# Two pairs of projection groups of a hybrid encoder layer as seven block products each, ahead of the attention heads

## The chip, the cores and the metric

The kernel runs on one core of one Trainium2 chip. The metric is the device time of one execution in microseconds (us). Its engines have one instruction queue each and start their instructions in the order of the program: TensorE (PE) multiplies matrices and writes PSUM, VectorE (DVE) and ScalarE (ACT) work element by element and read PSUM, GpSimd (POOL) works element by element on SBUF, and SyncE (SP) issues most DMAs. An instruction that waits for another engine holds up all that stand behind it in its own queue.

## The reference: what is computed

The layer takes x (512 tokens, 1024 channels, float32), normalises it, and multiplies it with one wide matrix `w_in` whose columns belong to two token mixers and two merge gates.

```python
h = rmsnorm(x, norm_w)
proj = jnp.einsum('bsd,de->bse', h, w_in) + b_in
(mq, mk, mv, mi, mf, mo, mz, sq, sk, sv, sz, gates) = jnp.split(proj, split_at, axis=-1)
# A: matrix memory, 4 heads of 256: causal conv + silu on mq, mk; chunkwise recurrence with
#    gates mi, mf; per-head rms norm; times sigmoid(mo) * silu(mz)            -> y_m
# B: stick-breaking attention, 8 heads of 128: rms norm on sq, sk per head;
#    a = sigmoid(z) * prod(1 - sigmoid(z) of the keys between), strictly causal;
#    a @ sv, times silu(sz)                                                   -> y_s
g_m, g_s = jnp.split(jax.nn.sigmoid(gates), 2, axis=-1)
merged = g_m * (y_m @ w_proj_m) + g_s * (y_s @ w_proj_s)
x = x + merged @ w_out
```

All of it is float32. The kernel keeps that accuracy by splitting each operand of a product into a high part in the fp32r type and a low remainder, and by adding three products: high-high, high-low and low-high.

## The kernel before

**Units.** All dense products are cut into 118 units, which one loop at the end of the function runs in order (L1263). A unit of `w_in` has 512 KB of weights: 1024 rows by 128 columns for a group whose result has channels on partitions (`chan_group`, L132), or 256 rows by 512 columns for a token-major group (`tok_group`, L148), in which four units add up to four token blocks of 128 by 512 in four PSUM banks. Either way a unit is 24 matmuls with 512 moving columns. Token-major groups are the q, k and V of the stick-breaking sets (two sets of four heads, `SbSet`) and the V of the matrix-memory pairs (`MPair`). The first four units (q of set 0) run with a code of their own (L1208), token block by token block, while x is still being normalised and transposed into `hh` and `hl`, the high and low parts of h, with 8 slices of 128 channels by 512 tokens each.

**What an iteration c of the loop does, in this order:** take the list `later[c]`; evacuate unit c-1; run the functions of the list; `ahead(c)`, which splits the weights of all units up to c+2 (ACT copies the high part, DVE subtracts to get the low part, L96) and lets SP load those up to c+4; first half of the matmuls of unit c; one step of each active head, and the start of a head that is due; second half of the matmuls. `AHEAD, LOADS = 2, 4` set the two distances. In iterations 1 to 3 the split comes first. Since every engine keeps program order, the place in this list is the place in each queue.

**later and defer.** `later[c]` holds what has been put off to iteration c, in the order in which it was entered; `defer(n, fn)` enters fn n iterations on. Three constants place the gate work: `gates_prep` (L575) fills the stationary tile `wg` on DVE in iteration 2, `gates` (L583) issues 16 matmuls against `wg` in iteration 4, before unit 4, and `gates_scan` starts in iteration 35.

**Heads.** A head is a generator that is advanced one step an iteration, except in the iterations of `REST`. Attention heads start in the iterations of `SB_START`, matrix heads in those of `M_START`, and not before their keys are done.

**q and k of a set.** The evacuation adds the bias row (L364); then `norm` takes four squares with a sum on ACT and the reciprocal root on POOL (L274, L275); k is scaled on DVE (L386) an iteration later. `turn` (L399) transposes 32 by 32 blocks on DVE, an iteration later `move` issues 16 DMAs (for set 0 all on SP, L415) which put the blocks in place, and two iterations after that q is weighted (L419).

**Buffers.** Tiles take buffers by tag; the numbers are in `BUFS` (L70). Those that matter here: `stg` 3 (loaded weights), `wh` and `wl` 3 each (split weights), `A` 4 and `P5` 2 (4 KB a partition each), `acc` 1 (2 KB, also the scratch of the squares), `tmp` 2, `qk` 9, `vl` 5, `y` 16.

**The tail.** The last product, with `w_out`, already runs as seven block products of two units each (`Product`, L1039). These halves have 12 matmuls of 512 columns.

Of the kernel before, what the change touches and what calls it, by code (L numbers as in the profile page):

```python
# [8 lines left out]
F32 = mybir.dt.float32  # L9
# [26 lines left out]
def tile_hybrid_layer(  # L36
# [157 lines left out]
    later = {}  # L194
    now = [0]

    def defer(n, fn):
        later.setdefault(now[0] + n, []).append(fn)

# [66 lines left out]
    def bias(ct):  # L266
        return bvec[:, ct:ct + 1]
# [68 lines left out]
    class SbSet:  # L336
        def __init__(self, s):
            self.s = s
            self.raw = {"q": [], "k": []}
            self.r = []  # L340
            self.v = []
            self.tz = {}

        def z_group(self):
            def evac(ct, ps):
# [9 lines left out]
        def qk_group(self, name, c0):  # L355
            row = []

            half = []

            def evac(tb, ps):  # L360
                if tb % 2 == 0:
                    half.extend(two("qk", name=name + "raw"))
                t = half[tb]
                nc.vector.tensor_tensor(t, ps, row[0], op=OP.add)  # L364
                self.raw[name].append(t)

                def norm():
                    ssq = tiny.tile([128, 4], F32, name="ssq", bufs=2)
                    rr = tiny.tile([128, 8], F32, name="r" + name, bufs=8 if name == "q" else 4)
                    r = rr[:, 0:4]  # L370
                    junk = blk("acc", BF, (128,), name="sqj")
                    for h in range(4):
                        nc.scalar.activation(junk, t[:, h * 128:(h + 1) * 128], AF.Square,
                                             accum_out=ssq[:, h:h + 1])
                    rstd(r, ssq, 128, EPS)
                    if name == "q":
                        rn = rr[:, 4:8]
                        nc.gpsimd.tensor_scalar(rn, r, -1.0, None, op0=OP.mult)
                        self.r.append((r, rn))
                        if tb == TB - 1:  # L380
                            defer(1, lambda: self.turn(name, 0))
                    else:
                        def scale():
                            for h in range(4):
                                hs = slice(h * 128, (h + 1) * 128)
                                nc.vector.tensor_scalar(t[:, hs], t[:, hs], r[:, h:h + 1], None, op0=OP.mult)  # L386
                            if tb == TB - 1:
                                done.add(("k", self.s))
                                defer(1, lambda: self.turn(name, 1))
                        defer(1, scale)  # L390

                if tb < 2 or name == "q" and self.s == 0:
                    norm()
                else:
                    defer(1, norm)

            tok_group(w_in, c0 + 512 * self.s, h_sta, evac, name == "q" and self.s == 0, c0 + 512 * self.s, row)

        def turn(self, name, g):  # L399

# [24 lines left out]
                defer(2, lambda: self.turn(name, 1))  # L425


        def v_group(self):
            row = []

            def evac(tb, ps):
                t = blk("tmp")
                nc.vector.tensor_tensor(t, ps, row[0], op=OP.add)
                vh = blk("vh", FR, (576,))[:, 0:512]
                vl = blk("vl", FR)
                nc.scalar.activation(vh, t, AF.Copy)
                self.v.append((vh, vl))
                if tb == TB - 1:
                    done.add(("v", self.s))
                return lambda: nc.vector.tensor_tensor(vl, t, vh.bitcast(F32), op=OP.subtract)  # L440

            tok_group(w_in, C_SV + 512 * self.s, h_sta, evac, False, C_SV + 512 * self.s, row)

        def head(self, h):
            hs = slice(h * 128, (h + 1) * 128)
# [136 lines left out]

    def gates():  # L583
        def row(name, p=4):
            return blk("y", name=name, p=p)

        wg = wg_t[0]
        ps = att_ps()
        for k in range(KT):
            nc.tensor.matmul(ps, wg[:, k, :], hh[:, k, :], start=k == 0, stop=False)  # L590
# [78 lines left out]
    class MPair:  # L669
# [25 lines left out]
        def qk_group(self, name, c0, o):  # L695
# [36 lines left out]

            chan_group(w_in, c0 + 512 * self.p, 512, h_mov, evac, lambda: self.prev())

        def v_group(self):
            row = []

            def evac(tb, ps):
                t = blk("tmp", shape=(2, 256))
                nc.vector.tensor_tensor(t, ps.rearrange("p (h e) -> p h e", h=2),  # L740
                                        row[0].rearrange("p (h e) -> p h e", h=2), op=OP.add)

                vh = blk("vh", FR, (576,))
                vl = blk("vl", FR, (2, 256))
                nc.gpsimd.memset(vh[:, 256:258].bitcast(F32), 1.0)
                dh = vh[:, 0:516].rearrange("p (h e) -> p h e", h=2)[:, :, 0:256]
                nc.scalar.activation(dh, t, AF.Copy)
                self.v.append((vh, vl))
                return lambda: nc.vector.tensor_tensor(vl, t, dh.bitcast(F32), op=OP.subtract)

            tok_group(w_in, C_MV + 512 * self.p, h_sta, evac, False, C_MV + 512 * self.p, row)

# [109 lines left out]
    sets = [SbSet(0), SbSet(1)]  # L862
    pairs = [MPair(0), MPair(1)]
    sets[0].qk_group("q", C_SQ)
    sets[0].qk_group("k", C_SK)
    sets[0].v_group()
    sets[0].z_group()
    sets[1].qk_group("q", C_SQ)
    sets[1].qk_group("k", C_SK)
    sets[1].z_group()  # L870
    sets[1].v_group()
    for p in pairs:
        p.o_group()
        p.z_group()
        p.v_group()
        p.qk_group("q", C_MQ, 0)
        p.qk_group("k", C_MK, 8)

    gs_t, gm_t = [], []

    def gs_tile(ct):
        if ct < 4:
# [3 lines left out]
            gs_t.extend(two("qk", name="gs"))  # L886
        return gs_t[ct]

    def gm_tile(ct):
        if ct % 2 == 0:  # L890
            gm_t.extend(two("qk", name="gm"))
        return gm_t[ct]

    def gate_group(c0, o, tile_of):
        def evac(ct, ps):
            nc.scalar.activation(tile_of(ct), ps, AF.Sigmoid, bias=bias(o + ct))

        chan_group(w_in, c0, D, h_mov, evac)

    gate_group(C_GS, 48, gs_tile)  # L900
    gate_group(C_GM, 40, gm_tile)
    n_gates = len(units)

    big = {}
# [330 lines left out]
    for p in (0, 1):  # L1235
        for h in range(2):
            pend.append((M_START[2 * p + h], 1,
                         lambda p=p: ("mk", p) in done, lambda p=p, h=h: pairs[p].head(h)))

    for k in range(5):  # L1240
        later.setdefault(n_gates - 1, []).append(y_early(k))
    for k in range(5, 8):
# [94 lines left out]
```

## Time and profile before

| what | value |
|---|---|
| median of 3 runs | 689.87 us (689.57 to 690.43) |
| profiled execution, first instruction to last (span) | 687.8 us; the page gives no other time of it |
| around the span, against the median | 2.1 us |
| granted TensorE clock | 1.000 |
| TensorE busy (matmuls) | 681.0 us, 99% |
| VectorE busy | 467.2 us, 68% |
| ScalarE busy | 337.1 us, 49% |
| GpSimd busy | 111.7 us, 16% |
| DMA | 84.74 MB, mean 123 GB/s |

Busy times are sums over one execution. A group of instructions stands as line, engine, operation, output and inputs by the program's names, and their shapes, then the count, the busy time, the mean of one in ns, and the idle time of the engine ahead of them with what ended most of it. Line numbers are those of the kernel before. Matmuls overlap: a duration of 0.39 us reaches into the next matmul, and the distance of two starts tells the rate.

### The profile page before, as it was taken

To read this page: it belongs to the slowest core of one execution; us is meant where nothing else is said; L and a number is where in the kernel's file an instruction comes from. 1 tells how busy PE (TensorE), PEld (TensorE's weight loads), DVE (VectorE), ACT (ScalarE), POOL (GpSimd) and SP (SyncE) were. 2 spreads that over 40 slices of the span, in tenths; PEclk is the share of its full clock that TensorE was granted. 3 is DMA by queue.
4 is the path that set the end of the run, shared out by engine and by line. 5 is a ranking of instruction groups with operands and counts; after the bars stand their busy time and mean duration, and the time that the engine had idled before them with its cause. 6 is when DMAs were issued, how large, how long until landed. Compare 5 with 4: busy or idle time off the path is not lost.

```text
span 687.8 us, 9389 instructions
## 1 busy us (share of the span) xinstructions
PE 681.0 (99%) x3162; PEld 568.9 (83%) x3162; DVE 467.2 (68%) x819; ACT 337.1 (49%) x631; POOL 111.7 (16%) x266
## 2 busy tenths in 40 slices
PE   8999999999999999999999999999999999999997
PEld 5888888888888888888888888888888888888876
DVE  6746787777997886789834648994352364445997
ACT  6245465566455653344466533448554343344451
POOL 4122042365430310000001210000112000111020
PEclk9999999999999999999999999999999999999999
DMA  7433543435463533643341343434223456599333
GB/s 250 139 95 107 160 138 105 134 112 149 134 171 86 124 111 83 139 95 92 107 117 53 107 109 85 128 91 134 68 64 90 115 176 200 141 206 205 121 82 103
DMA packets 122289, 84.74 MB, mean 123 GB/s; under 512 B 19018, under 2 KB 105956, under 8 KB 122240
## 3 DMA queue, kind: packets, MB, share of 16 engines
q1 hardware_dynamic: 119600, 77.97, 40.3%
q0 software_dynamic: 2496, 6.03, 4.7%
q8 instruction: 25, 0.41, 0.2%
q14 instruction: 24, 0.20, 0.1%
q10 hardware_dynamic: 144, 0.13, 0.1%
HBM read 66.22 MB, written 2.15 MB: 99 GB/s over the span
## 4 chain that ended last, share of the span: by engine, by line
PE 98%; DVE 1%; DMA 1%; SPq 0%; issue 0%; ACT 0%
PE dps L92 28%; PE dps L93 27%; PE dps L94 27%; PE aps L93 3%; PE aps L94 3%; PE aps L92 3%; PE dps L1216 1%; PE dps L1217 1%; PE dps L1218 1%; PE aps L811 1%; PE aps L813 1%; PE aps L812 1%; DMA stg<-in_w_in_dram 1%; PE aps L305 0%; DVE hl L317 0%; PE aps L591 0%
## 5 line engine op out<-in xcount | busy, mean ns | idle before, releaser
L98 DVE TENSOR_TENSOR wl<-stg,wh 128x1024 fp32r<-128x1024 f32 x92 | 112.5, 1223 | 106.0 <-ACT wh L97 105.5
L92 PE MATMUL dps<-hh,wh 128*128 128x512 f32 x448 | 175.0, 391 | 0.0
L94 PE MATMUL dps<-hh,wl 128*128 128x512 f32 x448 | 174.4, 389 | 0.0
L93 PE MATMUL dps<-hl,wh 128*128 128x512 f32 x448 | 174.4, 389 | 0.0
L97 ACT ACTIVATE wh<-stg 128x1024 fp32r<-128x1024 f32 x92 | 96.8, 1052 | 64.5 <-PE dps L94 44.3
L94 PEld LDWEIGHTS dps<-hh,wl 128*128 128x128 f32 x448 | 84.1, 188 | 17.7
L93 PEld LDWEIGHTS dps<-hl,wh 128*128 128x128 f32 x448 | 84.2, 188 | 16.8
L92 PEld LDWEIGHTS dps<-hh,wh 128*128 128x128 f32 x448 | 84.1, 188 | 16.7
L92 PE MATMUL dps<-wh,hh 128*128 128x512 f32 x224 | 87.7, 392 | 0.0
L94 PE MATMUL dps<-wh,hl 128*128 128x512 f32 x224 | 87.3, 390 | 0.0
L93 PE MATMUL dps<-wl,hh 128*128 128x512 f32 x224 | 87.2, 389 | 0.0
L94 PEld LDWEIGHTS dps<-wh,hl 128*128 128x128 f32 x224 | 42.0, 188 | 9.0
L92 PEld LDWEIGHTS dps<-wh,hh 128*128 128x128 f32 x224 | 42.1, 188 | 8.3
L93 PEld LDWEIGHTS dps<-wl,hh 128*128 128x128 f32 x224 | 42.1, 188 | 8.2
L704 DVE SCALAR_TENSOR_TENSOR acc<-tmp,vec,acc 128x511 f32<-128x511 f32 (+2 forms) x48 | 36.0, 750 | 1.7
L707 ACT ACTIVATE tmp<-acc 128x512 f32<-128x512 f32 x16 | 10.1, 633 | 50.8 <-DVE acc L704 50.8
L480 POOL TENSOR_SCALAR_AFFINE_SELECT om<-om 128x128 f32<-128x128 f32 x32 | 15.3, 479 | 96.2 <-ACT om L478 96.1
L486 DVE TENSOR_TENSOR_SCAN om<-om 128x512 f32<-128x512 f32 (+3 forms) x32 | 26.7, 834 | 5.5 <-POOL om L480 5.5
L764 POOL TENSOR_SCALAR_AFFINE_SELECT w_all<-om 128x128 f32<-128x128 f32 x16 | 5.3, 363 | 144.4 <-DMA om<-rb_d 144.4
L478 ACT ACTIVATE om<-aps,rq 128x512 f32<-128x512 f32 (+3 forms) x32 | 16.8, 524 | 21.0 <-PE aps L94 21.0
L94 PE MATMUL dps<-yh,wl 128*128 128x512 f32 x64 | 24.9, 389 | 0.0
L92 PE MATMUL dps<-yh,wh 128*128 128x512 f32 x64 | 24.9, 389 | 0.0
(249 smaller groups left out, 1217.8 us busy)
## 6 DMA issues: line engine op xcount, KB each, us to landing
stg<-in_w_in_dram SPq DMA_DIRECT2D x87, 512.0 KB, 3.9
az<-ay SPq DMA_DIRECT2D x128, 40.0 KB, 2.9
stg<-in_w_proj_s_dram SPq DMA_DIRECT2D x8, 512.0 KB, 4.7
B<-in_w_out_dram SPq DMA_DIRECT2D x8, 512.0 KB, 6.6
stg<-in_w_proj_m_dram SPq DMA_DIRECT2D x8, 512.0 KB, 5.9
wl<-stg POOLq DMA_DIRECT2D x8, 512.0 KB, 5.9
tz<-ty SPq DMA_DIRECT2D x72, 32.0 KB, 1.9
brow<-in_b_in_dram SPq DMA_DIRECT2D x8, 256.0 KB, 4.5
```

What stands on the lines that cost most here:

```text
L92: nc.tensor.matmul(ps, ah, bh, start=first, stop=False)
L93: nc.tensor.matmul(ps, ah, bl, start=False, stop=False)
L94: nc.tensor.matmul(ps, al, bh, start=False, stop=last)
L97: nc.scalar.activation(hi, src, AF.Copy)
L98: nc.vector.tensor_tensor(lo, src, hi.bitcast(F32), op=OP.subtract)
L478: nc.scalar.activation(om[:, 0:n], zp, AF.Sigmoid, scale=rn[:, h:h + 1])
L480: nc.gpsimd.affine_select(out=om[:, ts], in_=om[:, ts], compare_op=OP.is_gt, fill=1.0, base=0, channel_multiplier=1, pattern=[[-1, 128]])
L486: nc.vector.tensor_tensor_scan(back, back, back, 1.0, op0=OP.mult, op1=OP.bypass)
L704: nc.vector.scalar_tensor_tensor(acc[:, j:], t[:, 0:T - j], cw(3 - j, ch), acc[:, j:], op0=OP.mult, op1=OP.add)
L707: nc.scalar.activation(t, acc, AF.Sigmoid)
L811: nc.tensor.matmul(nm[:, 0:258], ph, vh, start=j == 0, stop=False)
L812: nc.tensor.matmul(sum_v, ph, vl, start=False, stop=False)
```

## The change

Four token-major groups leave their places: k and V of set 0, V of set 1, and V of matrix pair 0. They are taken two and two: (k of set 0, V of set 0) and (V of set 1, V of pair 0). A pair multiplies h with two blocks of 512 columns. With h cut into two halves of tokens and two of channels, and the weights into two halves of rows and the two column blocks, that is a product of 2 by 2 blocks, and the Winograd form computes it with seven block products in place of eight. Each block product is two units (`Half`) of 12 matmuls, so a pair has 14 units where there were 8 of 24. Both pairs run as units 4 to 31, ahead of the rest; E = 32.

- The sums of h (S1 to S4) are made once: `form_sum(2, i)` in iterations 2 and 3, S3 on POOL in 3 and 4, S1's split in 4 and 5, S3's split in 4 and 5, S4 in 6 and 7. The four weight blocks X, Z, Y, V of a pair are loaded in halves on SP, and the weight sums T2 and T1 (DVE), T3 and T4 (POOL) are made in place.
- Products accumulate on one another in PSUM where that gives the sums. A result that is needed twice is copied by ACT and added by a POOL DMA onto a tile that a DMA has filled with the bias row; the other part is added by DVE.
- The second pair's results go to DRAM (`v_park`) and come back 19 to 22 and 31 to 34 iterations after E. The first half of the gate group GM moves from the end to a place after z of set 1, and its results go to DRAM and back as well.
- The gate matmuls move from iteration 4 to 3; their preparation stays in iteration 2 and is entered in `later[2]` behind the form sum. The turns of q and k of set 0 get fixed places: iterations E - 7, E - 5 (by the deferral of 2) and E - 3. Heads start from E on.

```diff
+PAIRS = 2
+E = 4 + 14 * PAIRS
-SB_START = [10, 13, 16, 20, 26, 28, 32, 34]
-M_START = [52, 56, 70, 76]
-GATES_PREP, GATES_START, GATES_SCAN = 2, 4, 35
+SB_START = [E + n for n in (0, 2, 5, 8, 14, 16, 20, 22)]
+M_START = [E + n for n in (36, 40, 54, 60)]
+GATES_PREP, GATES_START, GATES_SCAN = 2, 3, E + 22
-REST = {11, 16, 20, 23, 24, 32, 44, 64}
+REST = {E + n for n in (4, 8, 11, 12, 48)}
...
+    def by_plan(s, name, fn):
+        if s:
+            defer(1, fn)
+        else:
+            later.setdefault(E + {"q": -7, "k": -3}[name], []).append(fn)
...
+    def form_sum(f, i):
+        if i == 0 and f != 3:
+            form_tiles(f)
+        if f == 2:
+            s1, t = flat("vl", "s1"), flat("acc", "st")
+            nc.vector.tensor_tensor(s1, h_part(hh, 1, 0, i), h_part(hh, 1, 1, i), op=OP.add)
+            nc.vector.tensor_tensor(t, h_part(hl, 1, 0, i), h_part(hl, 1, 1, i), op=OP.add)
+            nc.vector.tensor_tensor(s1, s1, t, op=OP.add)
+            s2 = flat("om", "s2")
+            nc.vector.tensor_tensor(s2, s1, h_part(hh, 0, 0, i), op=OP.subtract)
+            nc.vector.tensor_tensor(s2, s2, h_part(hl, 0, 0, i), op=OP.subtract)
+            sums[1, i] = s1
+            form_split(2, i, s2)
+        elif f == 1:
+            form_split(1, i, sums.pop((1, i)))
+        elif f == 3:
+            s3, t = flat("vl", "s3"), flat("tmp", "st")
+            nc.gpsimd.tensor_tensor(s3, h_part(hh, 0, 0, i), h_part(hh, 1, 0, i), op=OP.subtract)
...
+        else:
+            s4 = flat("acc", "s4")
...
+    class Half:
+        def load(self):
+            pass
+        def split(self):
+            self.wh = blk("wh", FR, (2, 512))
+            self.wl = blk("wl", FR, (2, 512))
+            name = {1: "X", 2: "Z", 6: "X", 5: "X", 7: "Y", 3: "V", 4: "Z"}[self.p]
+            split(self.pair.raw[name, self.g], self.wh, self.wl)
+        def mm(self, tb):
...
+            for i in range(2):
...
+                for n, (a, w) in enumerate(((sh, self.wh), (sh, self.wl), (sl, self.wh))):
+                    nc.tensor.matmul(pr.bank[key, tb], a, w[:, i, :], start=begin and n == 0,
+                                     stop=end and n == 2, skip_group_check=again)
...
+    class Pair:
...
+            b = self.base = len(units)
+            for p in (1, 2, 6, 5, 7, 3, 4):
+                for g in range(2):
+                    units.append(Half(self, p, g))
+            first = b == 4
+            for g in range(2):
+                if first:
+                    plan = {"X": g, "Z": g, "V": 1 + 2 * g, "Y": 2}
+                else:
+                    plan = {"X": b - 8 + g, "Z": b - 8 + 6 * g, "V": b - 4 + g, "Y": b - 6 + g}
+                for name, c in plan.items():
+                    self.at(c, self.load, name, g)
+                self.at(b + g, self.t3, g)
+                self.at(b + 1 + g, self.t2, g)
+                self.at(b + 2 + g, self.t4, g)
+                self.at(b + 4 + g, self.t1, g)
...
+        def put(self, key, q):
+            for tb in range(2):
+                u = blk("tmp", name="u")
+                nc.scalar.activation(u, self.bank[key, tb], AF.Copy)
+                nc.gpsimd.dma_start(out=self.dst[q][:, tb, :], in_=u, accum_op=OP.add)
+        def add(self, key, q):
+            for tb in range(2):
+                t = self.dst[q][:, tb, :]
+                nc.vector.tensor_tensor(t, self.bank[key, tb], t, op=OP.add)
+                self.got[q % 10](2 * (q // 10 - 1) + tb, t)
...
+    Pair(C_SK, C_SV, to_norm(0, "k"), to_parts(0))
+    Pair(C_SV + 512, C_MV, to_dram(0), to_dram(1))
...
+    for i in range(2):
+        at_unit(2 + i, form_sum, 2, i)
+        at_unit(3 + i, form_sum, 3, i)
+        at_unit(4 + i, form_sum, 1, i)
+        at_unit(6 + i, form_sum, 4, i)
...
+    for tb in range(TB):
+        at_unit(E + 19 + tb, from_dram, 0, tb, sets[1].v_parts)
+        at_unit(E + 31 + tb, from_dram, 1, tb, lambda tb, t: pairs[0].v_parts(tb, t)())
...
+    chan_group(w_in, C_GM, 512, h_mov, gm_early)
...
+    at_unit(n_gates + 3, gm_back)
+    for i in range(2):
+        at_unit(4 + i, s3_split, i)
```

More of the change, by code (lines that the diff above doesn't have):

```diff
@@ L584, in row @@
         def row(name, p=4):
-            return blk("y", name=name, p=p)
+            return blk("tmp", name=name, p=p)
         wg = wg_t[0]
@@ L864, in tile_hybrid_layer, with form_tiles, h_part, flat @@
     sets[0].qk_group("q", C_SQ)
-    sets[0].qk_group("k", C_SK)
-    sets[0].v_group()
+    form = {}
+    def form_tiles(f):
+        form[f] = [[blk("y", FR, (2, 256), name="form") for _ in range(2)] for _ in range(2)]
+        return form[f]
+    def h_part(t, row, col, i):
+        k = 4 * col + 2 * i
+        return t[:, k:k + 2, 256 * row:256 * row + 256].bitcast(F32)
+    sums = {}
+    def flat(tag, name):
+        return blk(tag, shape=(516 if tag == "om" else 512,), name=name)[:, 0:512].rearrange("p (k t) -> p k t", k=2)
@@ new lines, in to_norm, with to_parts, to_dram, from_dram @@
+    def to_norm(s, name):
+        return lambda tb, t: defer(1, lambda: sets[s].norm(name, tb, t))
+    def to_parts(s):
+        return lambda tb, t: defer(1 + tb % 2, lambda: sets[s].v_parts(tb, t))
+    v_park = [dp.tile([T, 512], F32, name="v_park") for _ in range(2)]
+    def to_dram(n):
+        return lambda tb, t: nc.sync.dma_start(v_park[n][128 * tb:128 * tb + 128, :], t)
+    def from_dram(n, tb, fn):
+        t = blk("brow", name="vback")
+        nc.sync.dma_start(t, v_park[n][128 * tb:128 * tb + 128, :])
+        later.setdefault(now[0] + 1, []).insert(0, lambda: fn(tb, t))
```

237 lines of the change are left out of this document (167 added, 70 removed).

## The prediction

> **What bounds the kernel now.** I read the page first, then busy times by stretch, then the timelines of the first 60 us.
>
> ```profile
> span 687.8 us, 9389 instructions
> PE 681.0 (99%) x3162; PEld 568.9 (83%) x3162; DVE 467.2 (68%) x819; ACT 337.1 (49%) x631; POOL 111.7 (16%) x266
> PE 98%; DVE 1%; DMA 1%; SPq 0%; issue 0%; ACT 0%
> ```
>
> TensorE bounds it: 99% busy, and 98% of the chain of waits. The page gives the profiled execution no time but its span, 687.8; the median of the runs is 689.87, so 2.1 us lie around the span, and I add them at the end.
>
> ```profile
> 14.30:37.00 22.70, 22.70 (x109) 18.66 (x108) 18.78 (x47) 7.17 (x26) 6.31 (x11) 1.00 0.35 107
> 180.00:200.00 20.00, 20.00 (x101) 17.03 (x100) 17.97 (x34) 10.89 (x20) 10.08 (x26) 1.00 0.51 140
> 640.00:660.00 20.00, 20.00 (x88) 16.06 (x87) 18.56 (x32) 12.01 (x20) 1.77 (x2) 1.00 0.28 77
> ```
>
> Columns: stretch, length, then busy us of PE, weight load, DVE, ACT, POOL, then clock. Even with DVE at 90% (17.97, 18.56 of 20) PE stands nowhere. So removed matmuls are time gained, unless something new makes PE wait.
>
> ```profile
> 1.50 4.11 PE L1184 MATMUL dps<-idle 128*128 128x512 f32 x9 [1.50 <-DVE idle L1179]
> 29.39 0.50 PE L1216 MATMUL dps<-fh,hh 128*128 128x512 f32 x1
> 34.98 0.39 PE L590 MATMUL aps<-hh,wg 128*128 128x512 f32 x1
> 38.61 0.39 PE L92 MATMUL dps<-wh,hh 128*128 128x512 f32 x1
> 44.05 0.39 PE L92 MATMUL dps<-wh,hh 128*128 128x512 f32 x1
> ```
>
> A duration (0.39) overlaps the next; starts count. One unit of 24 matmuls takes 44.05 - 38.61 = 5.44 us, 0.227 each; the 16 gate matmuls take 38.61 - 34.98 = 3.63.
>
> **What is removed.** Each pair of groups was 8 units of 24 (192 matmuls) and becomes 14 halves of 12 (168). Two pairs save 48 x 0.227 = **10.9 us**. This is firm: counts are in the code, and PE had no gaps.
>
> **What is added.** A half lasts 2.72 us but needs the same 128x1024 split as a whole unit:
>
> ```profile
> L98 DVE TENSOR_TENSOR wl<-stg,wh 128x1024 fp32r<-128x1024 f32 x92 | 112.5, 1223 | 106.0 <-ACT wh L97 105.5
> L97 ACT ACTIVATE wh<-stg 128x1024 fp32r<-128x1024 f32 x92 | 96.8, 1052 | 64.5 <-PE dps L94 44.3
> L386 DVE TENSOR_SCALAR kraw<-kraw,rk 128x128 f32<-128x128 f32 x32 | 6.6, 283 | 0.0
> L440 DVE TENSOR_TENSOR vl<-tmp,vh 128x512 fp32r<-128x512 f32 x8 | 5.5, 686 | 0.4
> L419 DVE TENSOR_SCALAR tz<-tz,qkw 128x1024 f32<-128x1024 f32 x4 | 3.0, 752 | 0.8 <-DMA tz<-ty 0.4 <-DMA stg<-in_w_in_dram 0.4
> ```
>
> In DVE starts (next fence) a 1024-wide operation costs 1.13 and a 512-wide one 0.61. Between unit 2 and unit E = 32 DVE gets 30 splits (33.9), 8 weight sums (9.0), 16 additions to the results (9.8), the form sums and their splits (24 x 0.61 = 14.6), and the rest of q, k, V and the gates, about 15 (half of the k and V rows, 3.3 and 2.7; turns and their weights, 5.6; additions of q and gate work, 3.4): 82 us. PE needs 5.44 + 3.63 + 28 x 2.72 = 85. DVE is thus nearly as full as PE, and a split is issued only two units (5.4 us) ahead: whatever makes DVE wait makes PE wait. I follow three places.
>
> **Place 1, the gates.** The gate matmuls move from unit 4 to unit 3, ahead of its matmuls in PE's order. They read `wg`, which DVE fills in the preparation at unit 2. That preparation was registered after the new form sum of unit 2, so DVE runs it behind five sums and a split.
>
> ```profile
> 28.53 1.13 DVE L317 SCALAR_TENSOR_TENSOR hl<-aps,nw_t,hh 128x128 fp32r<-128x128 f32 x4
> 29.57 1.21 DVE L98 TENSOR_TENSOR wl<-stg,wh 128x1024 fp32r<-128x1024 f32 x1
> 30.70 0.68 DVE L364 TENSOR_TENSOR qraw<-dps,brow 128x512 f32<-128x512 f32 x1
> 31.31 0.17 DVE L579 CAST wg<-gst 128x32 fp32r<-128x32 f32 x1
> 31.83 0.19 DVE L580 TENSOR_TENSOR wg<-gst,wg 128x32 fp32r<-128x32 f32 x1
> 31.48 0.31 ACT L373 ACTIVATE sqj<-qraw 128x128 bf16<-128x128 f32 x1 [6.17 <-DVE wg L579]
> 33.00 0.19 ACT L373 ACTIVATION_READ_ACCUMULATOR sqj<-qraw 128x1 f32 x1
> ```
>
> Nothing changes up to 31.31, since the sums need `hl`, finished at 29.57. Then: the first sum to 31.92; the second writes the only buffer of `acc`, which the four squares hold until 33.2; four sums to 35.65; ACT's copy (0.62) to 36.3, the low part to 36.9, the preparation (0.6, as 31.31 to 31.9 now) to 37.5. PE stands ready at 29.4: a stall of 8.1 us. Without the wait for `acc` and without hand-over times it is 6.8; with half a microsecond at each of three hand-overs 9.5. I take **8.1**.
>
> After it PE may restart slowly. The first row of the PE fence shows 9 matmuls after idleness at 0.457 each, double the later spacing. At that rate nine matmuls cost 2.1 more; at the warm rate none. A gap of 8 us is nearer the idle start than the gaps of up to 1 us in the trace, so **2.1**, with 0 to 2.1 for the range.
>
> The Trainium skill, "TensorE: Matmul & The Clock Gate", Part 1, says the clock halves after an idle window of some 3.4 us and recovers after as much activity, which speaks against any change that makes PE stand. By that page an estimate is 1.7 us here in place of 2.1. The half rate itself shows in the trace only at the start.
>
> **Place 2, pair 1.** PE leaves the gates at 37.5 + 3.6 + 2.1 = 43.2, unit 3 at 48.7, units 4 and 5 at 54.1. Unit 6 waits 0.4 for its split.
>
> ```profile
> L373 ACT ACTIVATE sqj<-qraw 128x128 bf16<-128x128 f32 x32 | 9.9, 310 | 19.1 <-DVE qraw L364 12.0 <-DVE wg L579 6.2
> L275 POOL TENSOR_TENSOR rq<-rq,mhalf 128x4 f32<-128x4 f32 x8 | 8.2, 1029 | 0.7
> 8.79 2.56 POOL L1166 TENSOR_TENSOR fl<-stg,fh 128x512 fp32r<-128x512 f32 x2 [2.57 <-ACT fh L1161]
> ```
>
> Unit 7's split stands on ACT behind the split of S3's second half, whose three sums are on POOL, behind Y's subtraction (T3) and behind the q norm of unit 3. From 48.7: q addition 0.65, four squares 1.75, POOL's norm 1.6 (1.03 is the power), T3 at 1024 wide 2.5 (twice the 1.28 of a POOL row), three sums 3.85: 59.0. Then ACT 0.62 and 1.05, DVE 1.15: 61.9. PE was ready at 57.2: 4.7. After that DVE's own queue sets the pace, against 2.72 a half:
> - unit 6 queues T2 (1.13), three sums for S4 (1.83), a split of 512 (0.62 + 0.61), then the split of unit 8 (0.4 more of ACT, 1.13): 5.7, loses 3.0;
> - unit 7 the same without T2, 4.6: 1.9;
> - units 8 and 9: T1 (1.13), ACT 1.05 and 1.13; then T1, two additions and 1.13: 3.3 and 3.5, lose 1.4;
> - unit 10: ACT has two copies and two norms (1.1 + 3.5) before its split: 2.7.
>
> With unit 6 and 0.1 at unit 11: 0.4 + 4.7 + 3.0 + 1.9 + 1.4 + 2.7 + 0.1 = **14.2**. Low end: DVE's bare work in units 4 to 11 (8 splits, 4 weight sums, 15 operations of 0.61, 8 k scalings at 0.21) is 24.4 against PE's 21.8: 2.6. High end: POOL half as slow again and each hand-over a little late, 20. Slow restarts at the shorter gaps are taken as nothing. The second pair has no form sums; its units come to 2 to 4 us of DVE with a lead of 5.4, and I charge nothing (if it falls behind as pair 1 did from unit 8, 4).
>
> **Place 3, the seam at unit 32.** The turns of q and k are fixed at units 25, 27 and 29, and each is followed by 16 DMAs on SP.
>
> ```profile
> L415 SPq DMA_DIRECT2D tz<-ty x72: 586/595/1699, 43.8 to 187.6; - x72
> 43.80 11.45 SPq L415 DMA_DIRECT2D tz<-ty  x16
> 55.35 1.04 SPq L117 DMA_DIRECT2D stg<-in_w_in_dram  x2
> 56.50 10.63 SPq L415 DMA_DIRECT2D tz<-ty  x16
> 42.36 1.42 DVE L405 STREAM_TRANSPOSE ty<-qraw 128x256 f32<-128x256 f32 x4
> stg<-in_w_in_dram SPq DMA_DIRECT2D x87, 512.0 KB, 3.9
> ```
>
> 16 issues take 10.5 us of SP. Before, four 5.44 us units of loads lay ahead; halves load nothing through the loop, so the load of unit 32 is issued at unit 28, behind two moves. From the start of unit 24: copies, split and turn on DVE to 4.7 (1.1 + 1.05 + 1.15 + 1.42); moves to 15.2 and 25.7; load issued 26.2, landed 30.1; split to 32.4. PE is there after 8 x 2.72 = 21.8: **10.6** (part shows as DVE waiting for the first move before it weights `tz`). If the turn runs 5 us sooner it is 5.6; with the third move ahead of unit 34 biting too, 13.
>
> **Costed at nothing.** V's and half of the gates' parking in DRAM: 14 DMAs more each way at most, fetched one unit (5.44) before use against 4 us of landing; uncovered, some 4 us each for the first of a group. The heads keep their operations; set 0's start over 8 units in place of 10, without V's work between them. The matrix heads keep their distances (4, 18, 24 units).
>
> Sum: 687.8 - 10.9 + 8.1 + 2.1 + 14.2 + 10.6 = 711.9; plus 2.1 gives **714.0**. With the low ends (6.8, 0, 2.6, 5.6) it is 694; with the high ones (9.5, 2.1, 24, 13) 728.
>
> **Rivals.**
> 1. Only the gates and the seam bite; pair 1's chains are absorbed while PE stands, as engines catch up: 711.9 - 14.2 + 2.1 = **700**. For it: the stretch 640 to 660 runs halves with DVE at 18.56 and PE at 20.00. Against: there the sums were made long before; here they queue with the splits.
> 2. Other side: order does not hurt, since DVE reaches each sum before PE needs the result, as busy sums suggest (PE about 670, DVE 467 + 41). Place: units 2 to 32. Price: all 10.9 kept, **679.0**. It decides if `wg` is ready by 29.4. Against: `hl` ends at 29.57, behind PE already.
> 3. Only the gates stall, and SP and DVE use that time: 687.8 - 10.9 + 10.2 + 2.1 = **689**, no change.
> 4. Set 0's closer heads make DVE the bound too: 17.97 per 20 us, packed 10 units into 8, is 22.5, 2.5 too much per 20, over 8 units (52 us with heads) 6.5: **720**.
>
> **Chances.** Forecast 0.57, rival 1 0.17, rival 2 0.11, rival 3 0.08, rival 4 0.07. A change under 0.2% (1.4 us) cannot be told from none. Rival 3 I split 0.03 faster, 0.04 same, 0.01 slower: faster 0.14, same 0.04, slower 0.82. The range 690 to 724 leaves out rival 2 and the tails.
>
> **What would show it.** PE should idle some 8 us before the first L590-like matmul, with DVE's preparation of `wg` as releaser; some 14 us in pieces of 1 to 5 before halves 7 to 13, released by DVE's low parts, with ACT waiting for POOL's sums once; some 10 us around unit 32, released by DVE behind a load that SP issued late. PE busy should fall near 670. I am wrong if `wg` is ready by 30 us, if PE runs gapless through pair 1, or if unit 32's load lands before unit 31 ends.

## The result, and the profile after

The changed kernel takes 754.7 us (median of 4 runs, 754.3 to 757.3) where the kernel before takes 690.0 (689.6 to 690.4): 1.0945 times as long, 95% interval 1.0927 to 1.0963. The forecast was 714.0 with a range of 690 to 724. The direction was right; the loss is 64.7 us in place of 24, and outside the range. The execution that was profiled is the longest of the four (757.3 us), so the stretches below add up to 3 us more than the medians differ by.

The head of the page, with the chain of waits:

```profile
span 755.5 us, 9487 instructions
PE 697.0 (92%) x3114; PEld 572.3 (76%) x3114; DVE 524.5 (69%) x863; ACT 358.3 (47%) x663; POOL 157.7 (21%) x292
PE 57%; DVE 3%; SPq 2%; ACT 1%; issue 1%; DMA 1%; POOL 0%; DVEq 0%; ACTq 0%; POOLq 0%
```

The 48 matmuls are gone (3114), yet PE's busy time rose from 681.0 to 697.0, its share of the chain of waits fell from 98% to 57%, and it now stands still for 58.5 us of the span (755.5 - 697.0), where it stood for 6.8. So there are two losses: waits, and slower matmuls between them. The timeline of PE, where it waited longest and where its stretches begin (start, duration, and in brackets the wait and its releaser):

```profile
37.95 0.77 PE L594 MATMUL aps<-hh,wg 128*128 128x512 f32 x1 [8.23 <-DVE wg L584]
43.29 0.40 PE L1448 MATMUL dps<-fh,hh 128*128 128x512 f32 x1
76.04 0.79 PE L958 MATMUL dps<-wh,form 128*128 128x512 f32 x1 [4.67 <-ACT wh L99]
99.98 0.39 PE L958 MATMUL aps<-wh,form 128*128 128x512 f32 x1
...
130.92 0.80 PE L958 MATMUL dps<-wl,form 128*128 128x512 f32 x1 [6.90 <-DVE wl L100]
160.05 0.47 PE L958 MATMUL dps<-wh,hh 128*128 128x512 f32 x1 [4.49 <-DVE dst L1033]
171.97 0.80 PE L94 MATMUL dps<-hh,wh 128*128 128x512 f32 x1 [4.60 <-ACT wh L99]
187.55 0.50 PE L94 MATMUL aps<-ktt,qtt 128*128 128x512 f32 x1 [3.71 <-ACT ktt L99]
209.06 0.39 PE L94 MATMUL dps<-wh,hh 128*128 128x512 f32 x1
388.43 0.50 PE L94 MATMUL aps<-ath,vh 128*128 128x512 f32 x1 [4.10 <-ACT ath L99]
```

These starts cut the span into five stretches. Unit 3 starts at 43.29, unit 14 at 99.98, unit 30 could start at 155.56 (160.05 less its wait of 4.49), unit 36 starts at 209.06. From each I take the time that it would last with PE at 0.227 us a matmul and never waiting: 33.0 to unit 3 (29.4 + 3.63), 32.6 for units 3 to 13, 43.5 for units 14 to 29, 31.5 for units 30 to 35 (5.44 for the halves, 26.06 for the rest, from the kernel of experiment 10, which ran them without a wait), and 536.2 for what is left of 687.8 - 10.9. What a stretch lasts beyond that:

| stretch | forecast | changed kernel |
|---|---|---|
| to unit 3 (gates) | 10.2 | 10.3 |
| units 3 to 13 (pair 1) | 14.2 | 24.1 |
| units 14 to 29 (end of pair 1, pair 2) | 0 | 12.1 |
| units 30 to 35 (seam) | 10.6 | 22.0 |
| behind | 0 | 10.2 |
| sum, less 10.9 | 24.1 | 67.7 (755.5 - 687.8) |

The gates came out as worked out; everything else was too low, and pair 2 and the end were not in the sum at all.

**What slowed VectorE.** Its timeline in pair 1, in pair 2 and at the seam:

```profile
53.90 3.31 DVE L100 TENSOR_TENSOR wl<-Z,wh 128x1024 fp32r<-128x1024 f32 x1 [0.18 <-ACT wh L99]
...
66.17 4.13 DVE L1009 TENSOR_TENSOR X<-X,Y 128x1024 f32<-128x1024 f32 x1
...
122.00 7.73 DVE L403 TENSOR_SCALAR dst<-dst,rk 128x128 f32<-128x128 f32 x8
...
156.11 0.75 DVE L429 TENSOR_SCALAR tz<-tz,qkw 128x1024 f32<-128x1024 f32 x1 [3.89 <-DMA tz<-ty]
```

and GpSimd's at the same times:

```profile
53.78 2.35 POOL L1005 TENSOR_TENSOR Y<-V,Y 128x1024 f32<-128x1024 f32 x1
56.10 2.26 POOL L907 TENSOR_TENSOR s<-hh 128x512 f32<-128x512 f32 x1
...
60.66 1.59 POOL L909 TENSOR_TENSOR s<-s,st 128x512 f32<-128x512 f32 x1
...
66.19 3.02 POOL L1013 TENSOR_TENSOR Z<-Z,X 128x1024 f32<-128x1024 f32 x1
...
122.98 5.29 POOL L1013 TENSOR_TENSOR Z<-Z,X 128x1024 f32<-128x1024 f32 x2
```

A low part that takes 1.22 us elsewhere takes 3.31 while GpSimd runs a sum; a weight sum takes 4.13; eight scalings that cost 0.28 each (2.2 by the rows of before) cost 7.73, and the 6.90 us wait of PE at 130.92 follows them. The sums on GpSimd are longer too: 2.26 for 512 wide where I had 1.28.

**What was late at the seam.** SyncE's queue (start, time in which it issued):

```profile
143.49 22.60 SPq L425 DMA_DIRECT2D tz<-ty x32
166.19 0.54 SPq L119 DMA_DIRECT2D stg<-in_w_in_dram  x1
...
170.29 10.93 SPq L425 DMA_DIRECT2D tz<-ty  x16
181.32 1.16 SPq L119 DMA_DIRECT2D stg<-in_w_in_dram  x2
```

The load of unit 32 stands behind two moves (22.60), as foreseen; the third move (10.93) then holds up the next two loads until 181.32. ACT waits 10.10 for one of these:

```profile
185.44 1.06 ACT L99 ACTIVATE wh<-stg 128x1024 fp32r<-128x1024 f32 x1 [10.10 <-DMA stg<-in_w_in_dram]
```

### The profile page after: what moved, and what is told of

Read it like the earlier page. It is cut to its first block, busy times and chain, and to the rows that moved or that the text cites. A ratio compares the mean times of both kernels' runs of the same rounds, so it can differ in the third digit from the quotient of the medians.

```text
span 755.5 us, 9487 instructions
## 1 busy us (share of the span) xinstructions
PE 697.0 (92%) x3114; PEld 572.3 (76%) x3114; DVE 524.5 (69%) x863; ACT 358.3 (47%) x663; POOL 157.7 (21%) x292
## 4 chain that ended last, share of the span: by engine, by line
PE 57%; DVE 3%; SPq 2%; ACT 1%; issue 1%; DMA 1%; POOL 0%; DVEq 0%; ACTq 0%; POOLq 0%
PE dps L94 16%; PE dps L95 16%; PE dps L96 16%; PE aps L95 2%; PE aps L96 2%; PE aps L94 2%; SPq L641 1%; SPq L526 1%; PE aps L817 1%; PE aps L819 1%; PE aps L818 1%; DMA az<-ay 1%; DVE wl L100 0%; DVE kraw L403 0%; DVE atl L100 0%
## 5 line engine op out<-in xcount | busy, mean ns | idle before, releaser
L94 PE MATMUL dps<-hh,wh 128*128 128x512 f32 x448 | 177.7, 397 | 4.6 <-ACT wh L99 4.6
L95 PE MATMUL dps<-hl,wh 128*128 128x512 f32 x448 | 176.6, 394 | 0.0
L100 DVE TENSOR_TENSOR wl<-stg,wh 128x1024 fp32r<-128x1024 f32 x76 | 92.8, 1221 | 81.2 <-ACT wh L99 81.1
L99 ACT ACTIVATE wh<-stg 128x1024 fp32r<-128x1024 f32 x76 | 80.0, 1053 | 66.4 <-DMA stg<-in_w_in_dram 34.3
L94 PE MATMUL dps<-wh,hh 128*128 128x512 f32 x96 | 37.5, 391 | 0.9 <-DVE qraw L373 0.9
L96 PE MATMUL dps<-wh,hl 128*128 128x512 f32 x96 | 37.4, 390 | 0.0
L95 PE MATMUL dps<-wl,hh 128*128 128x512 f32 x96 | 37.4, 390 | 0.0
L958 PE MATMUL dps<-wh,form 128*128 128x512 f32 x64 | 24.4, 458 | 5.9 <-ACT wh L99 5.9
L95 PE MATMUL dps<-yl,wh 128*128 128x512 f32 x64 | 24.9, 389 | 0.0
L958 PE MATMUL dps<-wl,form 128*128 128x512 f32 x32 | 15.1, 471 | 8.1 <-DVE wl L100 8.1
```

What stands on the lines that cost most here:

```text
L94: nc.tensor.matmul(ps, ah, bh, start=first, stop=False)
L95: nc.tensor.matmul(ps, ah, bl, start=False, stop=False)
L96: nc.tensor.matmul(ps, al, bh, start=False, stop=last)
L99: nc.scalar.activation(hi, src, AF.Copy)
L100: nc.vector.tensor_tensor(lo, src, hi.bitcast(F32), op=OP.subtract)
L958: nc.tensor.matmul(pr.bank[key, tb], a, w[:, i, :], start=begin and n == 0, stop=end and n == 2, skip_group_check=again)
```

## The experiments

Four suspects: the gates' stall; GpSimd holding VectorE up; SyncE's queue; the clock that PE is granted after a wait. Times are medians. In brackets stand the ratio to the kernel before, timed beside it (690.0 to 691.1), and its 95% interval. Line numbers are those of the kernel that was run, and run 4 means the run of experiment 4.

**1. The gates' preparation first.** Takes the stall at 37.95 away and leaves all else.

```diff
-    later.setdefault(GATES_PREP, []).append(gates_prep)
+    later.setdefault(GATES_PREP, []).insert(0, gates_prep)
```

> The preparation of wg is entered first in iteration 2, ahead of the form sum; nothing else changes. Theory 'queue order' (each wait stands by itself): wg is ready near 31.7 instead of 37.9, TensorE's gap before the gate matmuls falls from 8.2 to about 2 us and their slow start (5.3 us for 16 in place of 3.6) goes; the end comes 6 to 8 us earlier, about 747. Rival 'VectorE is the bound of units 2 to 13': what is gained at the gates is given back as longer waits in units 6 to 13, and the time stays at 752 to 755.

Measured: 754.2 us (1.0911, 1.0879 to 1.0943), 0.5 less, as the rival theory had it. PE's timeline:

```profile
31.61 0.66 PE L594 MATMUL aps<-hh,wg 128*128 128x512 f32 x1 [1.75 <-DVE wg L584]
...
53.39 0.79 PE L958 MATMUL aps<-wh,hh 128*128 128x512 f32 x1 [5.39 <-ACT wh L99]
...
99.50 0.39 PE L958 MATMUL aps<-wh,form 128*128 128x512 f32 x1
```

The gates wait 1.75 in place of 8.23, and a new wait of 5.39 follows; unit 14 starts at 99.50 in place of 99.98. The 6.4 us gained at unit 3 are given back within ten units, which fits a pace that VectorE, ScalarE and GpSimd set there, and not PE. One thing that I expected to go stayed: unit 3 starts at 36.95, so the 16 gate matmuls take 5.34 us behind a wait of 1.75 as well.

**2 and 3. The sums off GpSimd.** T3, T4 and S3 on VectorE (five lines, `nc.gpsimd` replaced; one is shown), or left out.

```diff
-            nc.gpsimd.tensor_tensor(z, z, x, op=OP.subtract)
+            nc.vector.tensor_tensor(z, z, x, op=OP.subtract)
```

> T3 and T4 (8 operations of 1024) and the three operations of S3 (6 of 512) run on VectorE instead of GpSimd. Theory 'contention' (a two-input GpSimd operation slows what VectorE does at the same time; VectorE's operations under them took 2.3 to 4.1 us in place of 1.2, and 8 scalings of k 7.7 in place of 1.7, about 20 us in all): VectorE's durations go back to 1.2 and 0.7, it pays 12.7 us for the sums and saves about 20; the time falls to 740 to 750. Rival 'queue order alone': VectorE, the fuller engine, gets 12.7 us more, and the time rises to 758 to 767.

> The sums on GpSimd are left out: T3 and T4 are the raw blocks Y and Z, and S3 is the raw part of h, so four of the seven products of each pair multiply other numbers. All else stays. Theory 'contention': the gaps at 57, 64, 66, 76 and 131 us shrink by about 15 us, the slow clock after them goes too, and the time falls to 720 to 732. Rival 'queue order alone': only the wait of ScalarE for S3 (4 us) and its slow start go, and the time is 745 to 750.

Measured: 741.1 us (1.0722, 1.0683 to 1.0760) and 732.2 (1.0592, 1.0561 to 1.0623). Giving VectorE more work made the kernel 13.6 us faster. Groups of VectorE between 29 and 215 us, first in the changed kernel (busy, mean ns):

```profile
L403 DVE TENSOR_SCALAR dst<-dst,rk 128x128 f32<-128x128 f32 x16 | 9.4, 667 | 0.0
L1009 DVE TENSOR_TENSOR X<-X,Y 128x1024 f32<-128x1024 f32 x4 | 8.9, 2214 | 0.0
```

then with the sums on VectorE:

```profile
L1009 DVE TENSOR_TENSOR X<-X,Y 128x1024 f32<-128x1024 f32 x4 | 4.9, 1217 | 0.0
...
L403 DVE TENSOR_SCALAR dst<-dst,rk 128x128 f32<-128x128 f32 x16 | 3.3, 280 | 0.0
```

The same operations take 1.22 and 0.28 us again, and the wait of 6.90 is 1.08. By the stretches, pair 1 falls from 24.1 to 17.6 and the next from 12.1 to 7.1. Without the sums they are 12.7 and 4.3. In pair 1 something else goes with the slow instructions: ScalarE's wait for S3, 7.89 us at 62.28, is 0.76 in the kernel with the sums on VectorE. These runs don't tell how the gain there divides between the two.

**4. The moves on two queues.** Half of the 16 DMAs of each move of set 0 are issued by GpSimd.

```diff
-                        q = nc.gpsimd if self.s and a % 2 else nc.sync
+                        q = nc.gpsimd if a % 2 else nc.sync
```

> Of the 16 DMAs of each move of set 0, 8 are issued by GpSimd instead of SyncE, as for set 1. Theory 'seam' (the loads of units 32 to 34 stand behind 32 and then 16 issues of 0.65 us): a move takes SyncE 5.2 us instead of 10.5, the load of unit 32 is issued about 10 us earlier, VectorE's waits for tz (3.9 and 4.9) and the gaps at 160, 172 and 188 us (4.5, 4.6, 3.7) go, with the slow clock behind them; the time falls by 12 to 18, to 737 to 743. Rival 'the loads themselves are late' (three stg buffers, 4 units ahead): the gaps stay within 3 us of what they are, and so does the time, 750 to 755.

Measured: 741.8 us (1.0731, 1.0696 to 1.0766), 13.0 less. The wait of 4.60 at unit 32 is gone, that of 3.71 is 0.40, and the stretch of units 30 to 35 loses 6.8 in place of 22.0; pair 1 (23.6) and the next (12.1) stay. The third move now takes 5.99 us of SyncE:

```profile
163.07 5.99 SPq L425 DMA_DIRECT2D tz<-ty  x8
```

**5. The gate scan one unit later.** In the changed kernel the scan starts in the unit in which the last head of set 0 starts (E + 22); before, one unit behind it. SyncE around the 4.10 us wait at 388:

```profile
372.31 6.85 SPq L641 DMA_DIRECT2D gfi<-l_d  x4
379.21 2.08 SPq L642 DMA_DIRECT2D gfi<-i_d  x1
381.34 4.94 SPq L526 DMA_DIRECT2D az<-ay  x8
```

```diff
-GATES_PREP, GATES_START, GATES_SCAN = 2, 3, E + 22
+GATES_PREP, GATES_START, GATES_SCAN = 2, 3, E + 23
```

> The change, with nothing but the gate scan put one unit later, behind the last head of set 0 and not in one unit with it. Theory that the 4.1 us gap at 388 us is the load of the gates standing ahead of that head's loads on SyncE: the gap goes, 749 to 752. Rival, that the head is late by itself: 753 to 757.

Measured: 749.7 us (1.0862, 1.0837 to 1.0888), 5.0 less. The gates' loads (6.85 and 2.08 us of issuing) had stood ahead of the head's eight; put behind it, the wait at 388 is gone.

**6. Three of these at once** (the edits of 2, 4 and 5), and **7.** with the preparation first as well.

> The change, with three of its costs taken away at once: the sums of the form on VectorE instead of GpSimd, half of the moves of set 0 issued by GpSimd instead of all by SyncE, and the gate scan one unit later. If the costs lie in different stretches of the time line they add up: 754.7 less 13.6 (sums, measured) less 13.0 (moves, measured) less 4.3 (the gap at 388) gives about 724; above 735 they overlap, and one stretch only hands its wait to the next. In either case it stays over the 690 of before, since VectorE still has the sums, the splits and the scalings to do in the same 130 us, unless the stall was GpSimd's and SyncE's alone, which would give 680 to 695.

> The change with the sums on VectorE, the moves on two queues, the scan one unit later (together 725.8), and the preparation of the gates first in its unit. In the change alone the last of these gave no gain, since the first pair's units used up what the gates no longer lost. If VectorE is still the bound in the first pair, the same holds: 722 to 728. If with the sums off GpSimd there is room now: 714 to 719, that is up to 8.2 less 1.75 us of the gap at the gates and the slow restart behind it.

Measured: 725.8 us (1.0503, 1.0465 to 1.0542) and 721.4 (1.0451, 1.0424 to 1.0479). The three single gains (13.6, 13.0, 5.0) would give 723.1: they lie mostly in different stretches and nearly add up. The fourth moves the losses by stretch from 11.7, 17.7, 6.7, 7.8, 4.4 to 2.6, 23.5, 5.2, 6.3, 4.9: of 9.1 gained at the gates pair 1 takes back 5.8. The medians differ by 4.4, and the two intervals overlap; 721.4 lies between what the two theories expected.

**8. What the form costs without GpSimd's sums.** The sums of GpSimd left out, and the three other edits.

> The change with the GpSimd sums left out altogether (so the blocks that need them hold other values and the output is another), half of the moves of set 0 issued by GpSimd, the gate scan one unit later and the gates' preparation first in its unit. Of the form only VectorE's own sums, splits and scalings are left. If these alone are more than TensorE's time in units 6 to 12: 708 to 718, with gaps left between 57 and 95 us. If what GpSimd and SyncE did was all of it: 680 to 692, that is 10.9 below before and no gap over 1 us ahead of unit 32.

Measured: 712.2 us (1.0315, 1.0294 to 1.0337). VectorE at unit 8:

```profile
56.79 0.68 DVE L910 TENSOR_TENSOR s<-hh,form 128x512 f32<-128x512 f32 x1
...
59.63 0.69 DVE L100 TENSOR_TENSOR form<-s,form 128x512 fp32r<-128x512 f32 x1 [0.70 <-ACT form L99]
60.57 1.23 DVE L100 TENSOR_TENSOR wl<-X,wh 128x1024 fp32r<-128x1024 f32 x1 [0.26 <-ACT wh L99]
61.72 0.68 DVE L910 TENSOR_TENSOR s<-hh,form 128x512 f32<-128x512 f32 x1
```

Three sums, a copy by ACT, two low parts, and the next three sums begin at 61.72: 4.93 us for a half that PE does in 2.72. So even with no sum on GpSimd the form loses 16.2 in pair 1 and 4.1 behind it, 20.3 against 10.9 saved. Of the 16.2, 4.29 is one wait of PE at 51.05, for a copy by ScalarE that stands behind the squares of q; so this is the price of the chain through both engines, and not of VectorE alone.

**9. The order alone.** The four groups ahead of the heads by ordinary units of eight block products, with the parking in DRAM, and no form (E = 20). The sums of h are left out, and the gates go back to unit 4; a part of the edit:

```diff
-    Pair(C_SK, C_SV, to_norm(0, "k"), to_parts(0))
-    Pair(C_SV + 512, C_MV, to_dram(0), to_dram(1))
+    sets[0].qk_group("k", C_SK)
+    v_tok(C_SV, lambda tb, t: sets[0].v_parts(tb, t))
+    v_tok(C_SV + 512, to_dram(0))
+    v_tok(C_MV, to_dram(1))
```

> The four token-major groups are computed ahead of the heads, as in the change, early results waiting in DRAM, but each by the ordinary four units with eight block products: no sums of the form, no three sums at the end, 20 units ahead of the heads, the same count of matmuls as before. Theory that the seven products' sums and scalings cost the time: 690 to 697, the seam hidden under ordinary units of 5.44 us each. Rival, that the changed order alone (moves, loads and first scores at once at the seam) costs it: 705 to 715, with gaps of 10 us or more at unit 20.

Measured: 709.2 us (1.0279, 1.0244 to 1.0315). I expected 690 to 697, with the seam hidden under units of 5.44: it isn't. **10.** The same with the moves on two queues and the scan one unit later:

> The kernel with the four groups ahead of the heads by ordinary units (709.2, 18.5 over before), with half of the moves of set 0 issued by GpSimd and the gate scan one unit later. Theory that what the order cost was the queue of SyncE, in which loads stand behind 16 moves at a time: the 8.1 us of gaps between 108 and 144 us, the slow matmuls behind them and the 2.2 us gap at 339 go, 691 to 697. Rival, that the order costs by VectorE or by the first scores coming at once: 702 to 709, with gaps of the same size released by VectorE while its splits are not waiting for a load.

Measured: 692.8 us (1.0038, 1.0023 to 1.0052). SyncE in the first of the two:

```profile
109.43 10.92 SPq L424 DMA_DIRECT2D tz<-ty  x16
120.45 1.16 SPq L118 DMA_DIRECT2D stg<-in_w_in_dram  x2
...
122.93 10.19 SPq L424 DMA_DIRECT2D tz<-ty  x16
```

and PE in the second, which runs the units of the seam without a wait (26.06 us, used above):

```profile
125.63 0.39 PE L93 MATMUL dps<-hh,wh 128*128 128x512 f32 x1
...
151.69 0.39 PE L93 MATMUL dps<-wh,hh 128*128 128x512 f32 x1
```

So 16.4 us of the new order were moves standing ahead of loads on one queue, and the scan (the two were changed together); what is left of it is 2.8. The order and the form together, with all four edits, take 721.4: against 692.8 the form adds 28.6 us where it was to save 10.9.

**11. The clock.** After its waits PE runs slower: busy times by stretch (PE, weight load, DVE, ACT, POOL, then clock, DMA share and GB/s) of the changed kernel show a granted clock of 0.81.

```profile
60.00:100.00 40.00, 27.61 (x89) 19.38 (x88) 30.52 (x32) 17.07 (x34) 17.62 (x15) 0.81 0.41 93
```

The experiment fills the waits with matmuls that change no result: 36 before the gates, 13, 26, 34, 14 and 28 before units 6, 7, 8, 9 and 23, 18 before unit 32.

```diff
+            fill = {6: 13, 7: 26, 8: 34, 9: 14, 23: 28}.get(now[0], 0) if tb == 0 else 0
...
+            for _ in range(fill):
+                nc.tensor.matmul(pr.bank[key, tb], zero, hh[:, 0, :], start=first, stop=first, skip_group_check=True)
...
```

> The change, with matmuls added that add nothing (a stationary of zeros, into the same sums; 36 before the gates, 13, 26, 34, 14 and 28 before units 6, 7, 8, 9 and 23, and 18 before unit 32), so that TensorE does not stand still in the gaps it had there. Theory that the clock was the second cost: the spacing stays near 0.227 us where it was 0.43, and 8 to 18 us of the 26.9 us of longer matmuls go: 737 to 747. Rival, that VectorE sets the pace there and the slow matmuls only fill time in which TensorE would have waited anyway: the idle time of the first 130 us grows by what the matmuls get shorter, 750 to 760.

Measured: 761.2 us (1.1016, 1.0988 to 1.1044). Its clock and its PE timeline:

```profile
60.00:100.00 40.00, 37.53 (x158) 29.17 (x157) 30.26 (x32) 17.01 (x34) 18.17 (x15) 1.00 0.39 92
```

```profile
41.99 0.39 PE L1458 MATMUL dps<-fh,hh 128*128 128x512 f32 x1
...
100.51 0.39 PE L968 MATMUL aps<-wh,form 128*128 128x512 f32 x1
...
130.70 0.79 PE L968 MATMUL dps<-wl,form 128*128 128x512 f32 x1 [6.90 <-DVE wl L100]
...
135.34 0.39 PE L961 MATMUL dps<-hh,zero 128*128 128x512 f32 x1
```

The clock is 1.00, the gates' matmuls are through 1.3 us earlier (41.99 against 43.29), and unit 14 starts at 100.51, not earlier than 99.98. In pair 1 the slow matmuls filled time in which PE would have waited: the low part of unit 12 begins on VectorE at 93.84 in place of 93.33, and PE waits 1.19 for unit 12 in both kernels. The 28 fillers of unit 23 came behind the wait that they were to cover (135.34, behind 130.70), which is where this kernel loses 5.0 more in the second stretch (17.1 against 12.1). Whether the clock costs something at the seam this run doesn't tell: of the 22.0 lost there the waits (4.49, 4.60, 3.71 and 0.96 at 189) are 13.8; the other 8.2 are slower matmuls between them (granted clock 0.84 from 155.56 to 209.06).

**12. The disputed cost by itself.** The kernel before, with 16 idle sums of 128x1024 on GpSimd in units 4 to 11, and nothing else.

```diff
+    spare = hp.tile([128, 2, 512], F32, name="spare", tag="spare")
+
+    def spare_sum(k):
+        nc.gpsimd.tensor_tensor(spare, hh[:, k:k + 2, :].bitcast(F32), hl[:, k:k + 2, :].bitcast(F32), op=OP.add)
+
+    for c in range(4, 12):
+        for k in (0, 2):
+            later.setdefault(c, []).append(lambda k=k: spare_sum(k))
```

> The kernel before, with nothing of the change, and 16 idle sums of 128x1024 from two SBUF tiles on GpSimd (two in each of units 4 to 11, their result is used by nobody). Theory that GpSimd and VectorE hold each other up when both read two SBUF operands: the mean of the eight splits on VectorE between 38.6 and 82.1 us rises from 1.23 us to 1.6 or more, that of the 16 scalings of k from 0.28 to 0.4 or more, GpSimd's sums take 2.0 to 3.0 us each, and the operations of VectorE that read PSUM stay at 0.68; the time stays within 3 us of before, since VectorE is busy for only 25 of 43.5 us there. Rival, that in the changed kernel it was the order of the queues: every VectorE row keeps its mean within 5%, and the time is the same as before.

Measured: 706.8 us (1.0235, 1.0216 to 1.0253). Groups between 38.6 and 82.1 us, of VectorE:

```profile
L98 DVE TENSOR_TENSOR wl<-stg,wh 128x1024 fp32r<-128x1024 f32 x6 | 14.5, 2423 | 6.3 <-ACT wh L97 6.3
L386 DVE TENSOR_SCALAR kraw<-kraw,rk 128x128 f32<-128x128 f32 x10 | 6.5, 709 | 2.8 <-POOL rk L275 2.8
L419 DVE TENSOR_SCALAR tz<-tz,qkw 128x1024 f32<-128x1024 f32 x2 | 5.8, 2902 | 0.0
L405 DVE STREAM_TRANSPOSE ty<-qraw 128x256 f32<-128x256 f32 x8 | 2.8, 407 | 0.0
L364 DVE TENSOR_TENSOR kraw<-dps,brow 128x512 f32<-128x512 f32 x4 | 2.5, 678 | 0.0
```

and of GpSimd:

```profile
L1228 POOL TENSOR_TENSOR spare<-hh,hl 128x1024 f32<-128x1024 f32 x12 | 33.3, 2774 | 0.8
```

The low parts go from 1.22 to 2.42, the scalings from 0.28 to 0.71, the weighting of `tz` from 0.75 to 2.90. The addition that reads PSUM (0.678, before 0.686) and the transposes (0.407, before 0.410) are untouched. This shows the mechanism with nothing of the change in the kernel. The time I had wrong (within 3 us of before): the reciprocal roots of k stand behind the idle sums on GpSimd, so k is scaled late, and PE waits for it:

```profile
82.20 0.48 PE L455 MATMUL aps<-ident,kraw 128*128 128x128 f32 x1 [6.80 <-DVE kraw L386]
```

So the 16.4 us of this kernel are no price of the contention alone.

No version beats the kernel before; the nearest to it has no form in it.

## Why the prediction was wrong, point by point

- **The saving.** 48 matmuls, as predicted. PE busy near 670 was wrong: 697.0, since matmuls behind the waits ran at a lower granted clock (0.81 in the stretch shown in experiment 11).
- **Place 1, the gates.** Stall 8.23 for 8.1, restart 1.7 for 2.1 (the 16 gate matmuls took 43.29 - 37.95 = 5.34 in place of 3.63). Here the estimate by the Trainium skill ("TensorE: Matmul & The Clock Gate", Part 1), 1.7, came out. But behind waits of 7.91, 8.45 and 8.03 in runs 2, 4 and 6 the same 16 matmuls took 5.89, 6.17 and 6.25, a restart of 2.3 to 2.6, so this doesn't decide between 1.7 and 2.1; and in run 1 the slow start came behind a wait of 1.75, which the Trainium skill's window of some 3.4 us doesn't explain. As a term of the sum the place was worth little: run 1 took 6.4 of it away for a gain of 0.5 (754.7 to 754.2). The step that failed is the adding up of places 1 and 2: while PE stands at the gates, VectorE and GpSimd work ahead on pair 1. Rival 1 had this thought, but took pair 1 to be absorbed whole: it lost 24.1 even so, and 30.0 with the wait at the gates down to 1.75 (run 1).
- **Place 2, pair 1.** 24.1 for 14.2. The step that failed is "T3 at 1024 wide 2.5, three sums 3.85: 59.0" and "T2 (1.13)": the three sums took from 56.10 to 62.25 (60.66 + 1.59), and the T2 that unit 6 queues took 4.13. The durations were those of engines that work alone. I priced GpSimd "half as slow again" for the high end, and never what it does to VectorE. With the sums on VectorE the stretch lost 17.6, with none 12.7; my 14.2 without the 4.7 for S3 is 9.5, so what is left of the chain was priced low as well, by about 3.
- **Place 2, pair 2.** "I charge nothing" was wrong: 12.1, of which 6.90 is one wait behind eight scalings that took 7.73. 5.0 of it goes with the sums moved to VectorE, and 4.3 stay without any sums; the 4 named for falling behind as in pair 1 is what should have been charged at the least.
- **Place 3, the seam.** The mechanism was right, and runs 4, 9 and 10 show it: the load of unit 32 went out 27.1 us behind the start of unit 24 (166.19 - 139.08), where I had 26.2. The size was off, 22.0 for 10.6. I let the third move bite only at the high end (13). It bit: the load behind it went out at 181.32 and PE waited another 3.71 and 0.96. And the wait of VectorE for the first moved blocks, which I had named and which took 3.89, came ahead of additions that PE needed, and cost it 4.49 ahead of unit 30 besides. The mis-sized term is this one: the waits on either side of unit 32, and the slow matmuls behind them, were left out.
- **Not in the sum: the end.** 10.2 behind unit 36. I wrote that the heads keep their operations, and did not follow the scan, which moved from one unit behind the last head's start into the same unit; 4.1 of wait, 5.0 by run 5. With the scan one unit later 4.1 of the 10.2 are still there (749.3 - 209.04 - 536.2); what they are stays open. It is a step that was moved past a queue, and SyncE's queue was not read for it.
- **Slow restarts at the shorter gaps as nothing.** The clock did fall (0.81 between 60 and 100 us), but run 11 shows that this cost nothing that counts in pair 1. For the seam it stays open.
- **The range.** It was made of the bounds of three places and had no room for a fourth cause. Its top, 724, also lies under the 728 of the high ends, and it leaves out rival 3 (689), which its sentence doesn't name. The largest single term that I had not looked for, GpSimd against VectorE, is 13.6 us by run 2; without it the changed kernel is still over the range (741.1), by the seam, the scan and what is left in pair 1.
- **The other rivals.** Rivals 2 and 3 fall with the stall at the gates and the 24.1 of pair 1. Rival 4 isn't borne out: between unit 36 and the wait at 388 PE has only two waits of 0.8 or more (0.91 and 0.80).

## What to carry to other kernels

The duration of an instruction in a trace holds for the neighbours that it had there: before work is put on GpSimd beside a busy VectorE, look which of VectorE's instructions read two SBUF operands or scale SBUF tiles, and price both engines' instructions as if they ran one after the other. When fewer matmuls are paid for with sums, compare the engine that makes the sums with PE unit by unit, not over the span: here a half had 2.72 us of PE and up to 4.93 of VectorE. And when work is put in another order, write out the queue that issues the DMAs: three moves of 16 small DMAs, ahead of the loads on one queue, cost 13.0 us by run 4, more than the 10.9 that the form could save.

## What the hardware showed that was not expected

GpSimd and VectorE hold each other up, but only in some instructions. A low part on VectorE with two SBUF operands took 1.22 us alone, 2.42 on the mean beside the idle sums and 3.31 in the changed kernel, where a weight sum of the same size took 4.13; a scaling of a 128x1024 SBUF tile by a column took 0.75 and 2.90; additions from PSUM and transposes kept their time. The excess of a single instruction (2.91 for the T2 of 4.13) is about one GpSimd sum (3.02). The Trainium skill has this: "GPSIMD Engine Reference", section 8, says that GpSimd shares its SBUF interfaces with VectorE, with contention for VectorE instructions with two SBUF inputs or in a mode that uses two ports, and "SBUF — State Buffer", section "SBUF: two separate sides", calls the shared port pair an exclusive lock on which the loser blocks for the whole instruction. The rows agree: one GpSimd sum is the excess, and what reads PSUM is spared. I had not used the rule for the forecast.

The second is how little the clock counted where another engine sets the pace: with fillers the granted clock went from 0.81 to 1.00 between 60 and 100 us, and unit 14 started no earlier.

The third is how short a gap can be that slows PE down. In run 1 a wait of 1.75 us was followed by 16 matmuls in 5.34 us (granted clock 0.68 between 31.6 and 37.0); in run 7 a wait of 2.06 was followed by the same 16 in 3.72, at a granted clock of 1.00. The length of one gap alone doesn't decide it here.
